# Seven products for eight: Strassen's method in the last block's up projection

## The chip, the cores and the metric

The kernel runs on one core of a Trainium2 chip. The metric is the device time of one execution in microseconds (us). TensorE (PE) multiplies, with weight loads (PEld) beside it; VectorE (DVE) and ScalarE (ACT) do elementwise work, GpSimd (POOL) some of it, and SyncE (SP) issues the DMAs between SBUF and DRAM. PE writes its results to PSUM, from where DVE and ACT take them.

## The reference

Three blocks run one after the other on a sequence of 1024 tokens of width 1024, all in float32. Two of their feed-forward parts are touched by the change. The first block's is a plain one; the third block's has a causal convolution of three taps between its two products and a gate:

```python
# first block
h2 = rms_norm(x, norm2_g[l])
up = jnp.square(jax.nn.relu(jnp.einsum('bsd,df->bsf', h2, w_up[l])))
x = x + jnp.einsum('bsf,fd->bsd', up, w_down[l])
...
# third block
def conv_ffn(h, w_up, conv_w, conv_b, w_down):
    u = h @ w_up
    C = u.shape[-1]
    u = lax.conv_general_dilated(
        u, conv_w.reshape(CONV_WIDTH_3, 1, C).astype(u.dtype), window_strides=(1,),
        padding=[(CONV_WIDTH_3 - 1, 0)], dimension_numbers=('NWC', 'WIO', 'NWC'),
        feature_group_count=C) + conv_b
    gate, val = jnp.split(u, 2, axis=-1)
    return (jax.nn.gelu(gate, approximate=True) * val) @ w_down
```

The rest (attention, retention, the mixed second block, the third block's attention and memory) is left as it was.

## The kernel before, in words

Activations lie as 8 tiles of 128 features, each over 1024 tokens, cut into two halves h of 512. A float32 product is made from three fp32r products: each operand is split into a high part (ACT rounds it: `whi`, `act`, `up`, `ws`) and a low part (the difference, on DVE or, with `pool_lo`, on POOL: `wlo` and the like), and `mm3` issues high x high, high x low and low x high. One dense unit (`dense`) is a 128-feature output chunk for one half: 8 x 3 = 24 matmuls of 128x512 into one PSUM bank. `chunk` loads a 512 KB weight chunk into `raw` and splits it into `whi` and `wlo`, two buffers of each; inside `third()` a third pair of `whi` and `wlo` is added in a pool of its own (`wx`).

The first FFN has 32 output chunks. Six are dense units, for h = 0 and then h = 1. The other 26 go in 13 Strassen units of two chunks: the two chunks are the rows of a 2 x 2 block matrix A, the two halves of the tokens the columns of B, and the inner dimension is cut in two. `right_forms` makes T1, T3 and T4 once, `left_forms` makes S1 to S4 of each unit (`sums`, split into `ws`), and `strassen` issues seven products of 4 x 3 = 12 matmuls, 84 a unit where dense units need 96. The four results are put together from PSUM by DVE additions (L820). `post` takes each: relu, square, and a write to DRAM (`upd`). The down product (`FfnDown`) reads `upd` back through two `nq` buffers, splits it, and runs over groups of 6, 6, 5, 5, 5, 5 chunks, each group adding its part to `acc`, which starts from x, loaded from `xd`.

The third FFN has 22 gate and 22 value chunks. `ffn` runs 6, 6, 5 and 5 pairs: for each half a gate unit, its convolution (ACT starts it with bias and the last tap, DVE adds two taps, and for h = 1 two small operations at the first columns with the `tail` of h = 0), gelu on ACT, a value unit, its convolution, the product on POOL, and the split into `up` in SBUF. The first group takes all of h = 0 first, since the norm of h = 1 (`join`, `norm_steps`) still runs beside it. Each group's down product follows it.

Nothing here writes the order of instructions by hand: a tile scheduler places each instruction on its engine's queue when the kernel is built, and slots, buffers and PSUM banks (six for products in a Strassen stage) decide what may start. Each engine then works through its queue in order.

## Time and profile before

| | |
|---|---|
| time, median of 3 runs | 3414.56 us (3406.56 to 3419.78) |
| profiled execution | 3415.66 us |
| its span, from the first to the last instruction | 3413.9 us |
| mean granted clock of TensorE | 0.975 |
| PE, PEld busy | 94%, 79% |
| DVE, ACT, POOL busy | 59%, 42%, 24% |
| first FFN (up and down) | about 580 to 1280 us of the span |
| third FFN (up and down) | about 2680 to 3390 us |

Matmuls are pipelined: one is shown about 0.39 us long, but the next starts earlier. The count of matmuls in a stretch, divided into its length, gives what one costs. A granted clock of 1.00 is TensorE's 2.4 GHz, 0.50 is 1.2 GHz.

### The profile page before, as it was taken

Reading aid. Unit: us, or ns where it says so; the run is one execution under the profiler, and the core shown is the slowest. Engines: PE = TensorE matmul, PEld = TensorE weight load, DVE = VectorE, ACT = ScalarE, POOL = GpSimd, SP = SyncE. Lnnn points to the kernel's source line nnn. Section 1 sums busy time; section 2 is a strip of 40 time slices with the busy share of each in tenths; the row PEclk is TensorE's granted clock in tenths of the full one; section 3 lists DMA queues with packets and bytes.
Section 4 is the critical chain, followed back from the end, with each engine's and each line's share of the span. In section 5 each row is a group of like instructions: output and inputs, shape, how many; then the busy total and the mean of one; then the engine's idle time right before and its main releaser. Section 6 shows DMA issues by size and latency. Waiting matters only on the chain.

```text
span 3413.9 us, 43231 instructions
## 1 busy us (share of the span) xinstructions
PE 3214.5 (94%) x16260; PEld 2679.9 (79%) x16260; DVE 2002.9 (59%) x3536; ACT 1427.8 (42%) x2512; POOL 822.2 (24%) x523
## 2 busy tenths in 40 slices
PE   7999999899999998789999899899999999999997
PEld 6789877788878887677667778778887888888886
DVE  8666566565443356975776566666636762434346
ACT  4454453454431124333644465655434542313132
POOL 3000024000000003521344444435333431201021
PEclk9999999999999999899999899999999999999999
DMA  4112134333352224345644122225322421111114
GB/s 129 46 52 63 51 112 160 121 121 114 127 183 81 78 70 154 99 123 179 203 162 135 59 63 67 82 86 177 131 68 99 154 85 58 45 50 46 51 43 149
DMA packets 144321, 348.18 MB, mean 102 GB/s; under 512 B 19441, under 2 KB 28017, under 8 KB 144113
## 3 DMA queue, kind: packets, MB, share of 16 engines
q1 hardware_dynamic: 144112, 345.42, 31.4%
q8 instruction: 128, 2.10, 0.3%
q14 instruction: 81, 0.66, 0.1%
HBM read 277.20 MB, written 61.34 MB: 99 GB/s over the span
## 4 chain that ended last, share of the span: by engine, by line
PE 40%; DVE 7%; issue 3%; ACT 3%; DMA 1%; POOL 1%; SPq 0%; DVEq 0%; POOLq 0%; ACTq 0%
PE ps_d L179 12%; PE ps_d L180 12%; PE ps_d L181 12%; ACT whi L143 1%; POOL wlo L145 1%; PE ps_s L1747 1%; PE ps_o L1330 1%; PE ps_t L1323 0%; DVE hE L1733 0%; DVE ssum L254 0%; DVE act L145 0%; DVE acc L1464 0%; DVE hSA L1748 0%; DVE wlo L145 0%; DVE acc L1465 0%
## 5 line engine op out<-in xcount | busy, mean ns | idle before, releaser
L179 PE MATMUL ps_d<-act,whi 128*128 128x512 f32 x1856 | 735.8, 397 | 22.7 <-ACT whi L143 10.2
L181 PE MATMUL ps_d<-act,wlo 128*128 128x512 f32 x1856 | 732.5, 395 | 17.4 <-DVE wlo L145 16.9
L180 PE MATMUL ps_d<-act,whi 128*128 128x512 f32 x1856 | 732.8, 395 | 0.1
L143 ACT ACTIVATE whi<-raw 128x1024 fp32r<-128x1024 f32 (+2 forms) x368 | 359.7, 978 | 779.9 <-PE ps_d L180 651.8
L145 POOL TENSOR_TENSOR wlo<-raw,whi 128x1024 fp32r<-128x1024 f32 (+1 forms) x162 | 391.1, 2418 | 747.2 <-ACT whi L143 712.9
L179 PEld LDWEIGHTS ps_d<-act,whi 128*128 128x128 f32 x1856 | 353.7, 191 | 100.7 <-ACT whi L143 17.2
L181 PEld LDWEIGHTS ps_d<-act,wlo 128*128 128x128 f32 x1856 | 353.2, 190 | 93.9 <-DVE wlo L145 20.9
L180 PEld LDWEIGHTS ps_d<-act,whi 128*128 128x128 f32 x1856 | 353.2, 190 | 72.7 <-issue 1.1
L179 PE MATMUL ps_d<-up,whi 128*128 128x512 f32 x864 | 337.2, 391 | 3.6 <-ACT whi L143 3.6
L181 PE MATMUL ps_d<-up,wlo 128*128 128x512 f32 x864 | 337.6, 391 | 1.7 <-DVE wlo L145 1.7
L180 PE MATMUL ps_d<-up,whi 128*128 128x512 f32 x864 | 337.0, 390 | 0.0
L145 DVE TENSOR_TENSOR wlo<-raw,whi 128x1024 fp32r<-128x1024 f32 (+2 forms) x206 | 230.2, 1117 | 168.1 <-ACT whi L143 164.7
L219 POOL TENSOR_TENSOR rr<-rv,mhalf 128x4 f32<-128x4 f32 (+1 forms) x43 | 46.4, 1080 | 716.4 <-DVE rv L209 530.2
L179 PE MATMUL ps_d<-mix,whi 128*128 128x512 f32 x512 | 200.1, 397 | 6.2 <-DVE acc L635 4.3
L181 PE MATMUL ps_d<-mix,wlo 128*128 128x512 f32 x512 | 200.8, 393 | 4.8 <-POOL wlo L145 4.8
L180 PE MATMUL ps_d<-mix,whi 128*128 128x512 f32 x512 | 202.3, 395 | 1.4 <-DVE mix L145 1.4
L179 PEld LDWEIGHTS ps_d<-up,whi 128*128 128x128 f32 x864 | 162.6, 188 | 38.5 <-ACT whi L143 4.9
L181 PEld LDWEIGHTS ps_d<-up,wlo 128*128 128x128 f32 x864 | 162.5, 188 | 36.9 <-DVE wlo L145 3.3
L180 PEld LDWEIGHTS ps_d<-up,whi 128*128 128x128 f32 x864 | 162.6, 188 | 33.9 <-DVE up L145 0.3
L179 PE MATMUL ps_d<-whi,act 128*128 128x256 f32 x512 | 151.4, 298 | 23.2 <-ACT act L379 16.0
L180 PE MATMUL ps_d<-wlo,act 128*128 128x256 f32 x512 | 150.2, 296 | 2.6 <-POOL wlo L145 1.6
L181 PE MATMUL ps_d<-whi,act 128*128 128x256 f32 x512 | 148.0, 292 | 0.1
(435 smaller groups left out, 6085.0 us busy)
## 6 DMA issues: line engine op xcount, KB each, us to landing
raw<-in_w_up SPq DMA_DIRECT2D x94, 512.0 KB, 3.4
raw<-in_w_fm SPq DMA_DIRECT2D x84, 512.0 KB, 3.4
raw<-in_w_out SPq DMA_DIRECT2D x42, 512.0 KB, 3.4
xd<-acc SPq DMA_DIRECT2D x80, 256.0 KB, 2.6
raw<-in_w_down SPq DMA_DIRECT2D x64, 320.0 KB, 3.0
nq<-upd SPq DMA_DIRECT2D x64, 256.0 KB, 3.0
acc<-xd SPq DMA_DIRECT2D x64, 256.0 KB, 5.7
raw<-in_w_down SPq DMA_DIRECT2D x32, 384.0 KB, 3.1
```

Of the source, the lines that this page charges most:

```text
L143: nc.scalar.activation(hi, src, AF.Copy)
L145: e.tensor_tensor(lo, src, hi.bitcast(F32), op=ALU.subtract)
L179: nc.tensor.matmul(out, lhsT=wh, rhs=xh, start=start, stop=False, skip_group_check=more)
L180: nc.tensor.matmul(out, lhsT=wh, rhs=xl, start=False, stop=False, skip_group_check=more)
L181: nc.tensor.matmul(out, lhsT=wl, rhs=xh, start=False, stop=stop, skip_group_check=more)
L219: self.nc.gpsimd.tensor_tensor(r, v, self.mhalf.broadcast_to([P, n]), op=ALU.pow)
L1330: nc.tensor.matmul(po[32 * hd : 32 * hd + 32, :P], lhsT=va[ct][:, band + kb, blk(hd, 32)], rhs=pts[hd][:, blk(kb)], start=kb == 0, stop=kb ...
L1747: nc.tensor.matmul(s[:, blk(j, 64)], lhsT=x[:, blk(j)], rhs=xv[:, nb * j : nb * j + nb, 1], start=True, stop=True)
```

## The change

First FFN. The next weight chunk is loaded before the current dense unit is issued. The left forms of the first Strassen unit are begun in the last two dense units of h = 1 (before: from the fourth on), in tiles c of the stage's pool. `strassen` issues the seven products in another order. The first, A11·B11, is copied by ACT from its bank into a second one, so that the next products add to it in PSUM; the next unit's A11·B11 is issued between S3·T3 and A22·T4. A unit has two DVE additions instead of five, and three ACT copies out of or within PSUM instead of one. The down product no longer starts from x: group 0 is copied, and x is loaded in 256 KB pieces and added at group 2.

Third FFN. Four pairs stay dense, h = 0 first, and 18 go through `strassen`, the gate chunk and the value chunk of a pair as the two rows. Convolution, gelu and the product (now on DVE) are in `post`; the result is written to DRAM (`upd3`) and read back by `FfnDown` with groups 6, 6, 5, 5. All `wlo` of this stage are made by DVE. The norm and the right forms work in place. `third()` is closed ahead of the stage and opened again for the down product alone.

```diff
         forms, left = iter(()), iter(())
-        for h in range(2):
-            if h == 1:
+        units = [(f, h) for h in range(2) for f in range(n0)]
+        wc = e.chunk(io["w1_up"][0])
+        for i, (f, h) in enumerate(units):
+            if i == n0:
                 for _ in steps:
                     pass
-                forms, left = right_forms(e, acc, hs, fm), left_forms(e, weight, 0, w)
-            for f in range(n0):
-                act(f, h, e.dense(e.chunk(io["w1_up"][f]), hs[h]), tmp.tile([P, HALF], F32, tag="c", name="c"))
-                next(steps, None)
-                next(forms, None)
-                if f >= 3:
-                    next(left, None)
-        hs = None
+                xs = [[a[:, j] for a in acc] for j in range(2)]
+                acc.clear()
+                forms, left = right_forms(e, xs, hs, fm), left_forms(e, weight, 0, w, tmp)
+            p = e.dense(wc, hs[h])
+            if i + 1 < len(units):
+                wc = e.chunk(io["w1_up"][units[i + 1][0]])
+            act(f, h, p, tmp.tile([P, HALF], F32, tag="c", name="c"))
+            next(steps, None)
+            next(forms, None)
+            if h and f >= n0 - 2:
+                next(left, None)
+        hs = p = None
...
-        def post(u, c):
-            for (i, h), t in c.items():
-                act(n0 + 2 * u + i, h, *t)
+        def post(u, i, h, p):
+            act(n0 + 2 * u + i, h, p, tmp.tile([P, HALF], F32, tag="c", name="c"))
...
-    def add(f, h, p, first):
+    def add(f, h, p, g):
         if len(acc) == f:
             acc.append(e.slot("acc"))
-            nc.sync.dma_start(acc[f], xd[f])
+        if g == 0:
+            nc.scalar.activation(acc[f][:, h], p, AF.Copy)
+            return
         nc.vector.tensor_tensor(acc[f][:, h], p, acc[f][:, h], op=ALU.add)
+        if g == 2:
+            t = e.tsq()
+            nc.sync.dma_start(t, xd[f, :, h])
+            nc.vector.tensor_tensor(acc[f][:, h], acc[f][:, h], t, op=ALU.add)
...
-    for i, tag in enumerate(("raw", "whi")):
+    for tag in ("raw", "raw") if tmp else ("raw", "whi"):
         a.append(e.wp.tile([P, NK, P], F32, tag=tag, name="raw"))
-        nc.sync.dma_start(a[i], weight(u, i))
+        nc.sync.dma_start(a[-1], weight(u, len(a) - 1))
     (a11, a12), (a21, a22) = ((t[:, :4], t[:, 4:]) for t in a)
-    s12, s34 = (e.wp.tile([P, 2, 4, P], F32, tag="wlo", name="sums") for _ in range(2))
+    def pair():
+        if tmp is None:
+            t = e.wp.tile([P, 2, 4, P], F32, tag="wlo", name="sums")
+            return t[:, 0], t[:, 1]
+        return [tmp.tile([P, HALF], F32, tag="c", name="c").rearrange("p (a b) -> p a b", a=4) for _ in range(2)]
     def put(name, t):
         y = e.slot("ws", (2, 4, P), F32R)
...
         w[name] = y
     put("A11", a11)
-    nc.vector.tensor_tensor(s12[:, 0], a21, a22, op=ALU.add)
-    nc.vector.tensor_tensor(s12[:, 1], s12[:, 0], a11, op=ALU.subtract)
-    put("S2", s12[:, 1])
+    s1, s2 = pair()
+    nc.vector.tensor_tensor(s1, a21, a22, op=ALU.add)
+    nc.vector.tensor_tensor(s2, s1, a11, op=ALU.subtract)
+    put("S1", s1)
     yield
+    put("S2", s2)
     put("A12", a12)
-    nc.vector.tensor_tensor(s34[:, 0], a11, a21, op=ALU.subtract)
-    put("S3", s34[:, 0])
     yield
-    put("S1", s12[:, 0])
+    s3, s4 = pair()
+    nc.vector.tensor_tensor(s3, a11, a21, op=ALU.subtract)
+    nc.vector.tensor_tensor(s4, a12, s2, op=ALU.subtract)
+    put("S3", s3)
+    yield
     put("A22", a22)
+    put("S4", s4)
     yield
-    nc.vector.tensor_tensor(s34[:, 1], a12, s12[:, 1], op=ALU.subtract)
-    put("S4", s34[:, 1])
-    yield
...
-    plan = (("A11", "B11", 0), ("S2", "T2", 1), ("A12", "B21", 0), ("S3", "T3", 1), ("S1", "T1", 2), ("A22", "T4", 1), ("S4", "B22", 2))
+    def product(p, w, a, b, start, last):
+        y, x = w.pop(a), fm.pop(b) if last else fm[b]
+        for k in range(4):
+            e.mm3(p, (y[:, 0, k], y[:, 1, k]), (x[k][:, 0], x[k][:, 1]), start and k == 0, k == 3, True)
+    def first(w, last):
+        ps = [e.pd() for _ in range(3)]
+        product(ps[0], w, "A11", "B11", True, last)
+        nc.scalar.activation(ps[1], ps[0], AF.Copy)
+        return ps
+    ps = first(w, n == 1)
     for u in range(n):
         last = u == n - 1
         nxt = {}
         pre = iter(()) if last else left_forms(e, weight, u + 1, nxt)
-        ps = [e.pd() for _ in range(3)]
...
-                p1 = e.tsq()
-                nc.scalar.activation(p1, ps[0], AF.Copy)
-                u2 = add(e.tnt(), ps[1], p1)
-                post(u, {(0, 0): (ps[0], new())})
-                u3 = add(new(), ps[1], p1)
-                u3 = add(u3, ps[2], u3)
-                post(u, {(1, 1): (u3, u3)})
-                p1 = add(p1, ps[1], p1)
-                post(u, {(1, 0): (p1, p1)})
-                u2 = add(u2, ps[2], u2)
-                post(u, {(0, 1): (u2, u2)})
...
+        def step():
+            next(pre, None)
...
+        product(ps[2], w, "S1", "T1", True, last)
+        c22 = e.tsq()
+        nc.scalar.activation(c22, ps[2], AF.Copy)
+        step()
+        product(ps[1], w, "S2", "T2", False, last)
+        c12 = e.tnt()
+        nc.scalar.activation(c12, ps[1], AF.Copy)
+        step()
+        product(ps[0], w, "A12", "B21", False, last)
+        post(u, 0, 0, ps[0])
+        step()
+        product(ps[1], w, "S3", "T3", False, last)
+        nc.vector.tensor_tensor(c22, ps[1], c22, op=ALU.add)
+        step()
+        follow = None if last else first(nxt, u + 2 == n)
+        product(ps[1], w, "A22", "T4", False, last)
+        post(u, 1, 0, ps[1])
+        post(u, 1, 1, c22)
+        step()
+        product(ps[2], w, "S4", "B22", False, last)
+        nc.vector.tensor_tensor(c12, ps[2], c12, op=ALU.add)
+        post(u, 0, 1, c12)
+        step()
+        w, ps = nxt, follow
     for _ in then:
         pass
-def ffn(e, groups, up_w, up, down_src, add, end, steps, per=1):
...
+    steps = join(1, ms, xs, g_cpost, g_fpre, xd3, hn[1], True)
+    third.close()
+    e.psum_split(d=6, s=0, o=0)
+    upd = e.dram.tile([22, P, 2, HALF], F32, name="upd3")
...
-    def up(f, h, ws):
-        cg = e.tsq()
-        conv(f, e.dense(ws[0], hs[h]), h, cg)
-        nc.scalar.activation(cg, cg, AF.Gelu_apprx_tanh)
-        cv = e.tnt()
-        conv(22 + f, e.dense(ws[1], hs[h]), h, cv)
-        nc.gpsimd.tensor_tensor(cv, cg, cv, op=ALU.mult)
-        y = e.slot("up", dt=F32R)
-        e.split(y[:, 0], y[:, 1], cv)
-        return y
-    def add(f, h, p, first):
+    def conv_rest(b, c):
+        c4 = lambda i: cw[:, 4 * b + i : 4 * b + i + 1]
+        t = tails.pop(b)
+        nc.vector.scalar_tensor_tensor(c[:, 0:1], t[:, 1:2], c4(1), c[:, 0:1], op0=ALU.mult, op1=ALU.add)
+        nc.vector.scalar_tensor_tensor(c[:, 0:2], t, c4(0), c[:, 0:2], op0=ALU.mult, op1=ALU.add)
+    def gelu(f, h, p, c):
+        conv(f, p, h, c)
+        if h:
+            conv_rest(f, c)
+        nc.scalar.activation(c, c, AF.Gelu_apprx_tanh)
+    def put_up(f, h, g, v):
+        nc.vector.tensor_tensor(v, g, v, op=ALU.mult)
+        nc.sync.dma_start(upd[f, :, h], v)
+    with ExitStack() as c2:
+        tmp = c2.enter_context(tc.tile_pool(name="str", bufs=8))
+        new = lambda: tmp.tile([P, HALF], F32, tag="c", name="c")
+        n0 = 4
+        fm, w = {}, {}
+        weight = lambda u, i: io["w3_up"][n0 + u + 22 * i]
+        forms, left = iter(()), iter(())
+        units = [(b, h) for h in range(2) for f in range(n0) for b in (f, 22 + f)]
+        wc = e.chunk(io["w3_up"][0])
+        for i, (b, h) in enumerate(units):
+            if i == 2 * n0:
+                for _ in steps:
+                    pass
+                forms, left = right_forms(e, xn, hs, fm), left_forms(e, weight, 0, w, tmp)
+            p = e.dense(wc, hs[h])
+            if i + 1 < len(units):
+                wc = e.chunk(io["w3_up"][units[i + 1][0]])
+            c = new()
+            if b < 22:
+                gelu(b, h, p, c)
+                cg = c
+            else:
+                conv(b, p, h, c)
+                if h:
+                    conv_rest(b, c)
+                put_up(b - 22, h, cg, c)
+            for _ in range(3):
+                next(steps, None)
+            next(forms, None)
+            if h and i >= len(units) - 2:
+                next(left, None)
+        hs = hn = p = c = cg = None
+        for _ in left:
+            next(forms, None)
+        for _ in forms:
+            pass
+        cs = {}
+        def post(u, i, h, p):
+            f = n0 + u
+            c = new()
+            if i == 0:
+                gelu(f, h, p, c)
+            else:
+                conv(22 + f, p, h, c)
+                if h:
+                    conv_rest(22 + f, c)
+            cs[i, h] = c
+            if i != h:
+                put_up(f, h, cs.pop((0, h)), cs.pop((1, h)))
+        down = FfnDown(e, (6, 6, 5, 5), upd, io["w3_down"])
+        strassen(e, tmp, fm, 22 - n0, weight, post, w, down.load(0))
+        fm.clear()
...
-    rest = ffn(e, (6, 6, 5, 5), lambda f: (e.chunk(io["w3_up"][f], pool_lo=True), e.chunk(io["w3_up"][22 + f])), up, io["w3_down"], add, end, steps_b, 4)
-    for _ in rest:
-        pass
-    third.close()
+    with e.third():
+        for _ in down.run(add, end):
+            pass
```

The scheduler sets the order anew, and three places of it are shown; the number behind a name is the buffer's. First, DVE in the first FFN, from the last `act` low parts (right forms, hs[1]) to the first left forms. Before:

```order
L145 TENSOR_TENSOR wlo_5878<-raw_5875,whi_5877 128x1024
L145 TENSOR_TENSOR wlo_5922<-raw_5919,whi_5921 128x1024
L145 TENSOR_TENSOR ws_6013<-raw_6007,ws_6013 128x512
L145 TENSOR_TENSOR wlo_5966<-raw_5963,whi_5965 128x1024
L787 TENSOR_TENSOR sums_6011<-raw_6009 128x512
L788 TENSOR_TENSOR sums_6011<-sums_6011,raw_6007 128x512
L145 TENSOR_TENSOR ws_6018<-sums_6011,ws_6018 128x512
L145 TENSOR_TENSOR act_6056<-acc_4750,act_6056 128x512
L145 TENSOR_TENSOR ws_6059<-raw_6007,ws_6059 128x512
L145 TENSOR_TENSOR wlo_6024<-raw_6021,whi_6023 128x1024
L792 TENSOR_TENSOR sums_6012<-raw_6007,raw_6009 128x512
L798 TENSOR_TENSOR sums_6012<-raw_6007,sums_6011 128x512
```

After:

```order
L145 TENSOR_TENSOR act_6048<-acc_4750,act_6048 128x512
L145 TENSOR_TENSOR wlo_5865<-raw_5862,whi_5864 128x1024
L145 TENSOR_TENSOR wlo_5909<-raw_5906,whi_5908 128x1024
L145 TENSOR_TENSOR wlo_5953<-raw_5950,whi_5952 128x1024
L145 TENSOR_TENSOR wlo_5997<-raw_5994,whi_5996 128x1024
L145 TENSOR_TENSOR wlo_6041<-raw_6038,whi_6040 128x1024
L145 TENSOR_TENSOR ws_6055<-raw_6051,ws_6055 128x512
L805 TENSOR_TENSOR c_6058<-raw_6053 128x512
L806 TENSOR_TENSOR c_6059<-c_6058,raw_6051 128x512
```

Five `wlo` of dense units now stand together ahead of the left forms (`ws`, and L805, which was L787).

Second, DVE in the third FFN, where h = 0 ends: `rv` and L263 are the norm of h = 1, L762 makes right forms, `act` is a split of hs[1], `wlo_22798` belongs to the second dense unit of h = 1. Before, from the first scaling of h = 1:

```order
L263 SCALAR_TENSOR_TENSOR nq_22605<-acc_21996,g_ffn_pre_norm_3_14910,ps_t_22600 128x512
L263 SCALAR_TENSOR_TENSOR nq_22610<-acc_21996,g_ffn_pre_norm_3_14910,ps_t_22600 128x512
L145 TENSOR_TENSOR act_22607<-nq_22605,act_22607 128x512
L145 TENSOR_TENSOR act_22612<-nq_22610,act_22612 128x512
L263 SCALAR_TENSOR_TENSOR nq_22694<-acc_21997,g_ffn_pre_norm_3_14910,ps_t_22600 128x512
L145 TENSOR_TENSOR up_22691<-nt_22659,up_22691 128x512
L263 SCALAR_TENSOR_TENSOR nq_22699<-acc_21997,g_ffn_pre_norm_3_14910,ps_t_22600 128x512
L1904 SCALAR_TENSOR_TENSOR nt_22758<-ps_d_22759,g_ffn_conv_3_14917,nt_22758 128x511
L145 TENSOR_TENSOR act_22696<-nq_22694,act_22696 128x512
```

After, from the norm's `rv` (L263 comes in four rows for eight operations):

```order
L207 TENSOR_REDUCE rv_22574<-ps_t_22569 128x4
L209 TENSOR_SCALAR rv_22574<-rv_22574 128x4
L263 SCALAR_TENSOR_TENSOR acc_22043<-acc_22043,g_ffn_pre_norm_3_14965,ps_t_22579 128x512 x2
L263 SCALAR_TENSOR_TENSOR acc_22044<-acc_22044,g_ffn_pre_norm_3_14965,ps_t_22579 128x512 x2
L263 SCALAR_TENSOR_TENSOR acc_22045<-acc_22045,g_ffn_pre_norm_3_14965,ps_t_22579 128x512 x2
L263 SCALAR_TENSOR_TENSOR acc_22046<-acc_22046,g_ffn_pre_norm_3_14965,ps_t_22579 128x512 x2
L145 TENSOR_TENSOR wlo_22798<-raw_22795,whi_22797 128x1024
L762 TENSOR_TENSOR acc_21191<-acc_22043,acc_21191 128x512
L1898 SCALAR_TENSOR_TENSOR c_22762<-ps_d_22731,g_ffn_conv_3_14972,c_22762 128x511
L762 TENSOR_TENSOR acc_21191<-acc_22043,acc_21191 128x512
L145 TENSOR_TENSOR act_22585<-acc_22043,act_22585 128x512
L762 TENSOR_TENSOR acc_21192<-acc_22044,acc_21192 128x512
```

The first `act` difference stood behind two scalings, and now stands behind eight, a `wlo`, sums of the right forms and a start of a convolution.

Third, ACT where the third FFN's down product begins. Before, the first `acc` copy of the first group and what is around it (`up` is the last split of the group):

```order
L143 ACTIVATE whi_23452<-raw_23450 128x768
L1903 ACTIVATE nt_23321<-ps_d_23322,g_ffn_conv_3_14917 128x512
L143 ACTIVATE up_23353<-nt_23321 128x512
L1929 ACTIVATE acc_23381<-ps_d_23362 128x512
L143 ACTIVATE whi_23499<-raw_23497 128x768
L1929 ACTIVATE acc_23381<-ps_d_23383 128x512
L1929 ACTIVATE acc_23428<-ps_d_23409 128x512
L143 ACTIVATE whi_23546<-raw_23544 128x768
```

After, from the last Strassen unit on (the tiles c_25932, c_25940 and c_25969 are its last results, `nq` the values read back, `whi_25994` the first weight in the reopened pool, whose space the tiles c had):

```order
L143 ACTIVATE up_25948<-nq_25946 128x512
L143 ACTIVATE up_25953<-nq_25951 128x512
L143 ACTIVATE up_25980<-nq_25978 128x512
L1897 ACTIVATE c_25932<-ps_d_25757,g_ffn_conv_3_14972 128x512
L1897 ACTIVATE c_25940<-sq_25832,g_ffn_conv_3_14972 128x512
L1897 ACTIVATE c_25969<-nt_25856,g_ffn_conv_3_14972 128x512
L143 ACTIVATE up_25985<-nq_25983 128x512
L1914 ACTIVATE c_25969<-c_25969 128x512
L143 ACTIVATE whi_25994<-raw_25992 128x768
L1981 ACTIVATE acc_26017<-ps_d_25998 128x512
L143 ACTIVATE up_26021<-nq_26019 128x512
L143 ACTIVATE up_26046<-nq_26044 128x512
```

Where weights were split ahead of the last results, the first weight's high part now stands behind the conv starts and the gelu of the last unit.

## Rows read from the trace of the kernel before

**Rows 1.** Page, part 1: engine busy us (share of the span) xinstructions.
```profile
PE 3214.5 (94%) x16260; PEld 2679.9 (79%) x16260; DVE 2002.9 (59%) x3536; ACT 1427.8 (42%) x2512; POOL 822.2 (24%) x523
```

**Rows 2.** Windows by stage: us, busy us (xinstructions) per engine, PEclk, DMA.
```profile
644.00:700.00 56.00, 50.64 (x207) 40.35 (x206) 28.07 (x42) 27.23 (x45) 0.00 (x0) 0.94 0.43 141
700.00:945.00 245.00, 245.00 (x1081) 202.65 (x1080) 131.74 (x200) 122.25 (x207) 0.11 (x1) 1.00 0.37 121
945.00:1000.00 55.00, 49.64 (x206) 38.97 (x205) 24.97 (x36) 14.53 (x22) 0.00 (x0) 0.97 0.55 181
...
2680.00:2780.00 100.00, 99.66 (x448) 82.02 (x447) 77.79 (x116) 49.16 (x69) 45.35 (x24) 1.00 0.34 115
...
3030.00:3390.00 360.00, 360.00 (x1594) 298.09 (x1592) 155.26 (x255) 101.16 (x138) 56.79 (x35) 1.00 0.21 66
```

**Rows 3.** PE waits, 560 to 1000: us in total, times, longest.
```profile
PE ps_d L179 <- ACT whi L143: 9.0, 7, 3.4
PE ps_d L181 <- DVE wlo L145: 5.4, 5, 3.2
```

**Rows 4.** PE waits, 2660 to 3394 (third FFN).
```profile
PE ps_t L228 <- POOL rr L219: 0.3, 1, 0.3
```

**Rows 5.** Windows behind two long PE waits; PEclk is the granted clock.
```profile
665.90:672.70 6.80, 6.28 (x15) 4.79 (x15) 0.61 (x1) 0.50 (x1) 0.00 (x0) 0.50 0.36 118
...
1290.50:1300.70 10.20, 4.83 (x12) 3.81 (x12) 9.80 (x14) 3.83 (x7) 3.18 (x3) 0.50 0.55 177
```

**Rows 6.** Lines by form, third FFN: busy us, mean ns of one, idle before.
```profile
L179 PE MATMUL ps_d<-act,whi 128*128 128x512 f32 x704 | 273.7, 389 | 0.0
...
L145 POOL TENSOR_TENSOR wlo<-raw,whi 128x1024 fp32r<-128x1024 f32 x29 | 69.9, 2410 | 304.2 <-ACT whi L143 304.2
...
L145 DVE TENSOR_TENSOR wlo<-raw,whi 128x1024 fp32r<-128x1024 f32 x28 | 34.4, 1229 | 41.2 <-ACT whi L143 38.2 <-PE ps_d L180 2.9
L1903 ACT ACTIVATE nt<-ps_d,g_ffn_conv 128x512 f32<-128x512 f32 x44 | 33.8, 768 | 31.0 <-PE ps_d L181 31.0
...
L1904 DVE SCALAR_TENSOR_TENSOR sq<-ps_d,g_ffn_conv,sq 128x511 f32<-128x511 f32 x44 | 32.8, 745 | 24.6 <-ACT sq L1903 24.6
...
L145 DVE TENSOR_TENSOR up<-nt,up 128x512 fp32r<-128x512 f32 x44 | 30.4, 691 | 77.0 <-ACT up L143 77.0
...
L143 ACT ACTIVATE up<-nt 128x512 fp32r<-128x512 f32 x44 | 27.8, 631 | 133.5 <-POOL nt L1920 133.5
...
L143 ACT ACTIVATE whi<-raw 128x768 fp32r<-128x768 f32 x16 | 13.5, 846 | 53.4 <-PE ps_d L180 53.4
...
L1912 DVE SCALAR_TENSOR_TENSOR nt<-tail,g_ffn_conv,nt 128x2 f32<-128x2 f32 x22 | 4.5, 206 | 0.0
```

**Rows 7.** DVE timeline in the opening of the third FFN: start us, length us.
```profile
2736.99 1.21 DVE L145 TENSOR_TENSOR wlo<-raw,whi 128x1024 fp32r<-128x1024 f32 x1
2738.13 0.74 DVE L1904 SCALAR_TENSOR_TENSOR sq<-ps_d,g_ffn_conv,sq 128x511 f32<-128x511 f32 x1
2738.79 1.28 DVE L145 TENSOR_TENSOR act<-nq,act 128x512 fp32r<-128x512 f32 x2
2739.99 0.68 DVE L145 TENSOR_TENSOR up<-nt,up 128x512 fp32r<-128x512 f32 x1
...
2743.53 1.30 DVE L145 TENSOR_TENSOR act<-nq,act 128x512 fp32r<-128x512 f32 x1 [0.16 <-ACT act L143]
```

**Rows 8.** POOL timeline, same stretch.
```profile
2741.87 2.41 POOL L145 TENSOR_TENSOR wlo<-raw,whi 128x1024 fp32r<-128x1024 f32 x1 [5.02 <-ACT whi L143]
```

**Rows 9.** Page, part 6: DMA issues, KB each, median us to landing.
```profile
xd<-acc SPq DMA_DIRECT2D x80, 256.0 KB, 2.6
...
nq<-upd SPq DMA_DIRECT2D x64, 256.0 KB, 3.0
acc<-xd SPq DMA_DIRECT2D x64, 256.0 KB, 5.7
```

More of the change, by code (lines that the diff above doesn't have):

```diff
@@ L675, in block1 @@
         save_x(f, 1)
-    steps = e.norm_steps([a[:, 1] for a in acc], g2, EPS, hs[1], inplace=True)
+    steps = e.norm_steps([a[:, 1] for a in acc], g2, EPS, hs[1], 2, inplace=True)
     e.psum_split(d=6, s=0, o=0)
@@ L850, in strassen @@
                     next(then, None)
-        for _ in pre:
-            pass
-        w = nxt
+        product(ps[2], w, "S1", "T1", True, last)
[22 more added lines that the diff above has]
+        w, ps = nxt, follow
     for _ in then:
         pass
-def ffn(e, groups, up_w, up, down_src, add, end, steps, per=1):
-    f0 = 0
-    for g, n in enumerate(groups):
-        us = [[], []]
-        fs = range(f0, f0 + n)
-        order = [(f, h) for h in range(2) for f in fs] if g == 0 else [(f, h) for f in fs for h in range(2)]
-        for f, h in order:
-            if g == 0 or h == 0:
-                w = up_w(f)
-            if h == 1:
-                for _ in steps:
-                    pass
-            us[h].append(up(f, h, w))
-            for _ in range(per):
-                next(steps, None)
-        last = g == len(groups) - 1
-        order = [(f, h) for h in range(2) for f in range(NK)] if last else [(f, h) for f in range(NK) for h in range(2)]
-        for f, h in order:
-            if last or h == 0:
-                w = e.chunk(down_src[f][:, f0 : f0 + n], (n, P))
-            add(f, h, e.dense(w, us[h]), g == 0)
-            for _ in range(per):
-                next(steps, None)
-            if last and f == NK - 1:
-                for _ in steps:
-                    pass
-                steps = end(h)
-        f0 += n
-    return steps
 class FfnDown:
@@ L1806, in join @@
         yield from add_x(e, ms, xs, g, r, [dst[k, :, h] for k in range(NK)], True)
-        yield from e.norm_steps(ms, g_next, EPS3, out, 1)
+        yield from e.norm_steps(ms, g_next, EPS3, out, 1, inplace)
     ms1 = tiles8(e)
@@ L1926, in add @@
+    def add(f, h, p, g):
         if acc[f] is None:
             acc[f] = e.slot("acc")
-        if first:
+        if g == 0:
             nc.scalar.activation(acc[f][:, h], p, AF.Copy)
```

45 lines of the change are left out of this document (11 added, 34 removed).

## The prediction

> **What bounds the kernel now.** I read the engine shares first [rows 1]: PE is busy 94% of the span, DVE 59% and ACT 42%, so PE's work and PE's waits make the time. Then the table by stage [rows 2]. Third FFN, from 3030 on: PE is busy all of 360 us at the full clock (2.4 GHz), and 360.00 / 1594 matmuls = 0.2258 us each. PE's waits in the whole stage sum to 0.3 us [rows 4]. So there time is the number of matmuls: that stage can gain only by fewer matmuls and lose only by new waits. First FFN: its Strassen units (700 to 945) have no gap, its two ends have. 207 matmuls x 0.2258 = 46.7 us stand in 56 us before them, 206 x 0.2258 = 46.5 in 55 us behind them: 9.3 and 8.5 us lost. The waits name ACT's whi and DVE's wlo, up to 3.4 and 3.2 us [rows 3]. An idle PE also lost clock: the grant was 0.50 (1.2 GHz) for 6.8 us after the longest of them, and for 10.2 us behind a wait in the second block [rows 5]. In 6.8 us it did 15 matmuls where 30 fit: 3.4 us.
>
> The sums stand against the profiled execution (3415.66 us, its span 3413.9 and 1.8 around it); the median is 1.1 lower.
>
> **Matmuls: -48.8 us.** Before, the third up product is 22 pairs x 2 rows x 2 halves x 24 = 2112 matmuls, three lines of 704 each (one of them in [rows 6]). After, 4 pairs stay dense (384) and 18 take seven products of 12 (18 x 84 = 1512): 216 fewer, x 0.2258 = 48.8 us.
>
> **Does DVE keep up in a Strassen unit? Taken: yes, 0 us.** PE needs 84 x 0.2258 = 19.0 us a unit. DVE gets 7 low parts and 4 sums of the weights, 2 PSUM additions and 2 products with gelu (15 of 128x512), 8 conv operations and 6 small ones (ends and tails). Back to back such operations start 0.60 us (128x512) and 0.66 us (conv) apart, though each is shown 0.68 and 0.74 long [rows 7]: 15 x 0.60 + 8 x 0.66 + 6 x 0.21 = 15.5 us, 82% of 19.0. With the mean lengths [rows 6] it is 15 x 0.69 + 8 x 0.745 + 6 x 0.21 = 17.6 us, 93%. Both fit. ACT gets 7 high parts, 3 PSUM copies, 4 conv starts and 2 gelus; at the longest of these lengths [rows 6], 16 x 0.77 = 12.3 us. POOL has nothing left in the stage, while before its work held DVE up: an act difference beside a POOL wlo took 1.30 us [rows 7, 8], where an up of the same size takes 0.69 on average [rows 6]. The Trainium skill ("SBUF — State Buffer", section "Who interferes with whom") has a reason: a DVE instruction with two SBUF inputs contends with a GpSimd one that reads SBUF. By that rule the lengths fall without POOL, and the trace's 1.30 beside 0.69 agrees.
>
> **The turn from h = 0 to h = 1: +20 us (bounds 4 and 28).** Before, 12 dense units (65 us) stood between the last cross-attention product and the first use of hs[1], and POOL made half of the wlo (29 beside DVE's 28 [rows 6]). Now there are 8 (8 x 24 x 0.2258 = 43.4 us), DVE makes every wlo (1.23 us [rows 6], 1.14 to the next start [rows 7]), and the right forms wait behind the same norm. As the order of DVE shows, behind the rv of the norm stand 8 scalings, a wlo, sums of the right forms and a conv start before the first act difference. I count from the first dense unit, with the spacings above: rv at 43.4; POOL's rr, its transposition and its spreading, an estimate of 3.0, to 46.4; 8 x 0.66 to 51.7; wlo to 52.8; four more to 55.4. PE has been done with h = 0 since about 45: about 10 us idle, then half clock. DVE then has ten operations to 61.4 (the other act parts, which units 9 and 10 take in turns), and 12 us of right forms, conv and products before the wlo of unit 11: 74.4. Without waits PE would have started that unit at 10 x 5.42 = 54.2. So 20 us are lost there; the half clock lies inside it, since DVE is late by itself. The lower bound is what remains if DVE's neighbours overlap better (a wait of 4 us); the upper adds 7 us for a second fall of the clock and the late wlo of unit 12.
>
> **The end of the Strassen units: +18 us (bounds 4 and 22).** down.run opens the third pair of weight buffers in the space that the tiles c had, and its first whi goes there. So that whi waits until the last products have been written to DRAM. The order of ACT shows it behind the three conv starts and the gelu of the last unit, and PE has nothing else to do. From the last Strassen matmul (0): two pairs of up values have yet to go through the two nq buffers in front of the conv starts on ACT, each turn 3.0 (transfer [rows 9]) + 0.63 + 0.69 = 4.3 us, of which half lies under PE's last 24 matmuls: 4.2. Three conv starts, six conv operations, two products and a low part follow on DVE to 11.9; the write of 256 KB, taken as 2.6 like xd<-acc [rows 9], to 14.5; whi 128x768 0.85 [rows 6] to 15.4. Then half clock for 6.8 us or more [rows 5]: +3. The lower bound is a write that lands early with nothing queued before it; the upper takes 10.2 us at half clock.
>
> **First FFN: -10 us (bounds 0 and -18).** At 644 to 700 the wlo of the last dense units stood between the left forms on DVE, and ACT's whi behind the ws of sums that waited for a weight. Now five wlo follow each other ahead of the left forms: I take 7 of 9.3 us. Behind the units, 8 loads acc<-xd (5.7 us each [rows 9]) leave SP's queue, but the two nq buffers still feed the up values one by one: 3 of 8.5 us. In the units DVE loses 3 of 5 additions and ACT gains 2 copies; PE has no gap there [rows 2], so 0. The stall at 621 to 627 hangs on norm and right forms, whose order stays: 0. The x values, added at group 2 by 16 loads and additions beside the down product: 0, for PE waits for nothing there; without that cover 16 x 0.69 = 11 us of DVE.
>
> **Sum:** -48.8 + 20 + 18 - 10 = -20.8: 3415.7 - 20.8 = 3394.9, and from the median 3393.8; I write 3394.
>
> **Rivals.** (A) Both new waits are small, since what DVE and SP have in front of them runs earlier than I count. For it: PE waits 0.3 us in the stage now, though DVE is busy 78 of 100 us at the same turn [rows 2, 4]. Against: the queues shown in the orders. 4 + 4 instead of 38: -48.8 + 8 - 12 = -53, 3362.
> (B) Not faster, no loss: the waits reach their upper bounds and the first FFN gives nothing: -48.8 + 28 + 22 = +1, 3415. For it: every row on the norm and nq chains has a wait behind it; against: three things must come together.
> (C) Slower: DVE becomes the bound inside the units. The place is the addition of S3·T3 (c22), which has to read its bank before A22·T4 may write there: if DVE is late, PE waits in every unit. 17.6 us by mean lengths leave 1.4 us for waits on ACT and PE at 16 handovers; 0.2 us each pass it. From 1.2 us of wait a unit (20.8 / 18) the gain is gone; at 2.5 it is 18 x 2.5 = 45: 3439. Against: DVE lengths overlap [rows 7]. The Trainium skill ("Perfetto Trace Analysis", "Identifying the Most-Contended Engine") takes the share of busy time as a fair measure of how near Vector is to its limit; by it 93% would leave almost nothing. Rows 7 disagree in size: starts are closer than lengths.
> (D) The change does not do what it says, the two halves' conv or the copies in PSUM undoing the saved products: 216 matmuls less are in the program, so only a wait could do it, and that is (C).
>
> **How the numbers follow.** Forecast 0.52, its own range 3378 to 3410; A 0.24; B 0.12; C 0.12. The measurement tells 0.5% (17 us) from no change, so faster means below 3397.5. Of the forecast some 0.30 lies below that and 0.22 above; A is all faster; B is the same, with 0.02 slower; C is 0.03 same and 0.09 slower. Faster 0.54, same 0.35, slower 0.11. The range leaves the lower part of A and most of C out: 3360 to 3420.
>
> **What would show it.** The matmul count of the third up product falls by 216 and its units hold 0.226 us a matmul: right on the first two steps; PE gaps at each addition of c22: C. Two gaps of about 10 us with the grant at 0.50 behind them, one 45 us after the stage's first matmul and one at the first down matmul, the second with PE waiting for ACT's whi and this for the write upd3<-c: right on the next two. Gaps under 3 us there would make the prediction wrong on the low side. In the first FFN the waits at 644 to 700 should be gone and those behind the units still be there.

## The result

The changed kernel takes 3396.8 us (median of 5 runs, 3391.8 to 3399.1) beside 3414.5: a ratio of 0.995 with the 95% interval 0.9936 to 0.9964, 12 to 22 us less. The forecast was 3394. The profiled execution took 3399.1 us with a span of 3397.3, against 3415.7 and 3413.9.

The profile after, engine shares first (as [rows 1]):

```profile
PE 3174.9 (93%) x16044; PEld 2645.4 (78%) x16044; DVE 2119.8 (62%) x3795; ACT 1504.1 (44%) x2710; POOL 698.0 (21%) x451
```

216 PE instructions are gone (16260 to 16044), DVE has 117 us more, POOL 124 less. The windows by stage, columns as in [rows 2]:

```profile
644.00:700.00 56.00, 54.92 (x241) 44.80 (x240) 30.69 (x46) 31.28 (x54) 0.00 (x0) 1.00 0.47 152
925.00:980.00 55.00, 55.00 (x245) 45.53 (x244) 14.16 (x19) 21.60 (x37) 0.11 (x1) 1.00 0.37 122
...
2714.00:2742.00 28.00, 15.21 (x57) 11.27 (x56) 27.11 (x44) 14.91 (x25) 0.12 (x1) 0.86 0.08 29
...
2780.00:3116.00 336.00, 334.71 (x1477) 276.83 (x1476) 272.08 (x512) 172.96 (x288) 0.00 (x0) 1.00 0.27 86
3116.00:3135.00 19.00, 6.02 (x17) 4.08 (x17) 11.77 (x23) 7.22 (x11) 0.00 (x0) 0.69 0.37 127
3134.48:3140.00 5.52, 5.52 (x13) 4.35 (x14) 0.94 (x1) 0.00 (x0) 0.00 (x0) 0.50 0.26 71
```

The first two are the ends of the first FFN's Strassen units: 241 matmuls in the 56 us that held 207, and behind the units 245 in 55 us, without a gap. The next three are the third FFN: at the turn of the halves 28 us hold 57 matmuls where 124 fit (28 / 0.2258), the Strassen units run at the full clock with DVE busy 272 of 336 us, and 19 us at their end hold 17 matmuls. The last is the half clock behind that. PE's waits in 560 to 1000 (us in total, times, longest; as [rows 3]) are left with the one at 622 that hangs on wlo, the two on acc at 580 and 599, which stood there before too, and small ones:

```profile
PE ps_d L181 <- DVE wlo L145: 3.2, 1, 3.2
PE ps_d L179 <- DVE acc L635: 3.0, 2, 2.2
PE ps_d L179 <- ACT whi L143: 0.9, 2, 0.5
```

In the third FFN, where PE waited 0.3 us in all [rows 4], these waits stand now (2655 to 3340):

```profile
PE ps_d L179 <- ACT whi L143: 12.8, 3, 11.0
PE ps_d L180 <- DVE act L145: 6.7, 1, 6.7
PE ps_d L181 <- DVE wlo L145: 3.9, 1, 3.9
PE ps_d L179 <- DVE sq L867: 1.9, 1, 1.9
PE ps_d L179 <- ACT act L143: 1.7, 1, 1.7
PE ps_d L179 <- ACT acc L1438: 1.5, 1, 1.5
PE ps_d L179 <- ACT ps_d L840: 1.3, 1, 1.3
```

**The turn.** DVE's timeline, start and length in us, at the 6.7 us wait on an act part and the 3.9 us one on a wlo:

```profile
2712.13 0.69 DVE L207 TENSOR_REDUCE rv<-ps_t 128x4 f32<-128x512 f32 x1
...
2714.89 5.36 DVE L263 SCALAR_TENSOR_TENSOR acc<-acc,g_ffn_pre_norm,ps_t 128x512 f32<-128x512 f32 x8 [1.87 <-PE ps_t L228]
...
2723.16 0.68 DVE L145 TENSOR_TENSOR act<-acc,act 128x512 fp32r<-128x512 f32 x1
...
2740.14 1.22 DVE L145 TENSOR_TENSOR wlo<-raw,whi 128x1024 fp32r<-128x1024 f32 x1
```

The rv comes 44.5 us after the first dense matmul (2667.68; forecast 43.4), the eight scalings begin 2.8 us later, the first act part follows at 2723.16, and unit 11's wlo at 2740.14, 17 us behind that, with DVE occupied nearly throughout. The dense units end at 2776.3: 108.6 us, of which 384 x 0.2258 = 86.7 are dense matmuls and 1.1 five early Strassen ones. The other 20.8 us are lost.

**The end.** ACT's timeline around the first down weight:

```profile
3122.73 0.63 ACT L143 ACTIVATE up<-nq 128x512 fp32r<-128x512 f32 x1 [0.91 <-DMA nq<-upd]
...
3130.13 0.63 ACT L1914 ACTIVATE c<-c 128x512 f32<-128x512 f32 x1 [3.95 <-DVE c L1908]
3133.59 0.84 ACT L143 ACTIVATE whi<-raw 128x768 fp32r<-128x768 f32 x1 [2.83 <-DMA upd<-c]
```

PE's timeline at the same place, its last Strassen matmul and its first down matmul:

```profile
3122.87 0.57 PE L181 MATMUL ps_d<-act,ws 128*128 128x512 f32 x1
3134.48 0.79 PE L179 MATMUL ps_d<-up,whi 128*128 128x512 f32 x1 [11.04 <-ACT whi L143]
```

The last up value ahead of the conv starts is split at 3122.73, these follow, then the gelu at 3130.13, and the whi waits 2.83 us for the write of c before it starts at 3133.59. PE stands from its last Strassen matmul (3122.87) to 3134.48 and then works at the half clock, 13 matmuls in 5.5 us. Before that it had waited 1.9 us for the addition of S3·T3 (L867, at 3118.09), which stood on DVE behind an up part that nq had delayed; first ACT's row, then DVE's:

```profile
3116.82 0.63 ACT L143 ACTIVATE up<-nq 128x512 fp32r<-128x512 f32 x1 [1.06 <-DMA nq<-upd]
...
3117.48 0.69 DVE L145 TENSOR_TENSOR up<-nq,up 128x512 fp32r<-128x512 f32 x1 [0.20 <-ACT up L143]
```

Together 1.9 + 1.6 (matmuls at half clock after it) + 11.2 (from one start to the next, less one matmul at that clock) + 2.6 (half clock behind it) = 17 us.

### The profile page after: what moved, and what is told of

Its sections match the earlier page's. It is cut to its first block, busy times and chain, and to the rows that moved or that the text cites. A ratio compares the mean times of both kernels' runs of the same rounds, so it can differ in the third digit from the quotient of the medians.

```text
span 3397.3 us, 43416 instructions
## 1 busy us (share of the span) xinstructions
PE 3174.9 (93%) x16044; PEld 2645.4 (78%) x16044; DVE 2119.8 (62%) x3795; ACT 1504.1 (44%) x2710; POOL 698.0 (21%) x451
## 4 chain that ended last, share of the span: by engine, by line
PE 35%; DVE 9%; ACT 3%; issue 2%; DMA 1%; POOL 1%; SPq 0%; DVEq 0%; ACTq 0%; POOLq 0%
PE ps_d L179 10%; PE ps_d L180 10%; PE ps_d L181 10%; ACT whi L143 1%; DVE act L145 1%; DVE acc L1454 1%; POOL wlo L145 1%; PE ps_s L1737 1%; DVE hE L1723 0%; DVE wlo L145 0%; DVE hSA L1738 0%; DVE acc L1455 0%; DVE pr L1650 0%; DVE ssum L254 0%; PE ps_o L1320 0%
## 5 line engine op out<-in xcount | busy, mean ns | idle before, releaser
L143 ACT ACTIVATE whi<-raw 128x1024 fp32r<-128x1024 f32 (+2 forms) x328 | 317.3, 968 | 711.6 <-PE ps_d L180 601.9
L179 PE MATMUL ps_d<-act,whi 128*128 128x512 f32 x1280 | 512.8, 401 | 24.5 <-DVE acc L316 8.1
L181 PE MATMUL ps_d<-act,wlo 128*128 128x512 f32 x1280 | 508.4, 398 | 20.4 <-DVE wlo L145 19.5
L180 PE MATMUL ps_d<-act,whi 128*128 128x512 f32 x1280 | 508.9, 398 | 6.8 <-DVE act L145 6.7
L145 POOL TENSOR_TENSOR wlo<-raw,whi 128x1024 fp32r<-128x1024 f32 (+1 forms) x134 | 326.0, 2436 | 446.4 <-ACT whi L143 427.9
L179 PE MATMUL ps_d<-act,ws 128*128 128x512 f32 x868 | 335.0, 390 | 3.8 <-DVE sq L867 1.9
L180 PE MATMUL ps_d<-act,ws 128*128 128x512 f32 x868 | 338.4, 390 | 0.0
L181 PE MATMUL ps_d<-act,ws 128*128 128x512 f32 x868 | 336.2, 390 | 0.0
L179 PEld LDWEIGHTS ps_d<-act,whi 128*128 128x128 f32 x1280 | 245.8, 192 | 80.8 <-ACT whi L143 14.6
L145 DVE TENSOR_TENSOR wlo<-raw,whi 128x1024 fp32r<-128x1024 f32 (+2 forms) x194 | 212.6, 1096 | 148.8 <-ACT whi L143 148.7
L181 PEld LDWEIGHTS ps_d<-act,wlo 128*128 128x128 f32 x1280 | 245.3, 192 | 73.9 <-DVE wlo L145 22.6
L180 PEld LDWEIGHTS ps_d<-act,whi 128*128 128x128 f32 x1280 | 245.7, 192 | 57.6 <-DVE act L145 7.5
L179 PEld LDWEIGHTS ps_d<-up,whi 128*128 128x128 f32 x864 | 163.0, 189 | 45.6 <-ACT whi L143 11.7
L179 PEld LDWEIGHTS ps_d<-act,ws 128*128 128x128 f32 x868 | 163.2, 188 | 38.7 <-ACT ps_d L840 2.7
L181 PEld LDWEIGHTS ps_d<-act,ws 128*128 128x128 f32 x868 | 163.3, 188 | 34.1
```

The lines of the kernel that those rows point to most:

```text
L143: nc.scalar.activation(hi, src, AF.Copy)
L145: e.tensor_tensor(lo, src, hi.bitcast(F32), op=ALU.subtract)
L179: nc.tensor.matmul(out, lhsT=wh, rhs=xh, start=start, stop=False, skip_group_check=more)
L180: nc.tensor.matmul(out, lhsT=wh, rhs=xl, start=False, stop=False, skip_group_check=more)
L181: nc.tensor.matmul(out, lhsT=wl, rhs=xh, start=False, stop=stop, skip_group_check=more)
```

## The experiments

Each was run beside the kernel before: the whole change in one series of measurements, the others in three more. The ratios and 95% intervals are those on record; the two medians of a row divide to within 0.0009 of them. The last two columns are lengths in us from one trace of each kernel: the first FFN from the wait at 622 to the one ahead of the second block, the third FFN from its first matmul to the end of the span. Where the code is the same they repeat well: the four kernels with the third FFN as in the whole change have 729.6 to 730.0.

| run | median us | before, same series | ratio | first FFN | third FFN |
|---|---|---|---|---|---|
| before | 3414.5 | | | 664.3 | 741.0 |
| whole change | 3396.8 | 3414.5 | 0.9950 [0.9936, 0.9964] | 647.7 | 729.6 |
| first_only | 3400.0 | 3410.9 | 0.9967 [0.9954, 0.9979] | 647.2 | 741.2 |
| third_only | 3406.1 | 3410.9 | 0.9983 [0.9973, 0.9992] | 661.3 | 729.6 |
| end_turn | 3383.7 | 3410.9 | 0.9921 [0.9908, 0.9933] | 647.6 | 719.5 |
| dense6 | 3397.8 | 3410.9 | 0.9959 [0.9945, 0.9972] | 647.8 | 730.0 |
| pool_lo | 3397.2 | 3412.1 | 0.9961 [0.9948, 0.9973] | 646.3 | 733.6 |
| no_sums | 3387.1 | 3412.1 | 0.9928 [0.9915, 0.9940] | 647.9 | 723.6 |
| end_lazy | 3376.6 | 3412.1 | 0.9896 [0.9881, 0.9911] | 647.4 | 712.3 |
| lazy_pool | 3382.4 | 3412.1 | 0.9913 [0.9900, 0.9927] | 647.2 | 715.9 |
| acc_load | 3398.2 | 3408.9 | 0.9962 [0.9945, 0.9978] | 649.7 | 730.0 |
| old_loop | 3398.5 | 3408.9 | 0.9961 [0.9946, 0.9975] | 653.6 | 729.8 |
| lazy5 | 3373.0 | 3408.9 | 0.9889 [0.9875, 0.9904] | 647.7 | 710.4 |

**The two parts apart.** first_only keeps the third block as before; third_only keeps block1 and its helpers.

> First FFN changed, third FFN as before. Theory (the first FFN's waits at both ends of its Strassen units go, 16 to 17 us in the traces, and the matmul count stays): 3414.5 - 17 = 3398 us, as fast as the whole change, with no PE gap over 1 us between 640 and 1260 us. Rival (part of these 17 us is the clock's luck in one execution, my forecast of -10 being right): 3405 us.

> Third FFN changed, first FFN as before. Theory (216 matmuls x 0.2258 = -49 us, then +21 at the turn of the halves and +18 at the first down matmul): 3414.5 - 10 = 3404 us, and the two PE gaps of about 7 and 11 us stand there again. Rival (the order in the untouched second and third block, which the scheduler laid anew, costs the 10 us that the whole change lost between the two FFNs): 3414 us, no gain at all.

first_only is 11 us faster (7 to 16), third_only 5 (3 to 9): together about the whole, 17. In time first_only lies nearer to its rival, and third_only between theory and rival. The traces side with the theory of first_only: the first FFN takes 647.2 us there, 647.7 in the whole change and 664.3 before. But third_only, whose first FFN has the instructions of before in the same order, took 661.3, so some 3 of these 17 us are chance of one execution. third_only shows the waits of 6.7 and 11.0 us again, and its third FFN is 11.4 us shorter than before, of which 5 are lost again just ahead of it ("Why the prediction was right"). Its rival does not hold: between the two FFNs its instructions come in the order of before, and this stretch, from the wait ahead of the second block to the last cross-attention, takes 1330.1 us there and 1334.1 before. So most of the 49 us that the third FFN saved in matmuls it gave back inside itself.

**The end.** end_turn moves the rotation of the weight buffers by one; end_lazy opens the pool after the third chunk.

```diff
 # end_turn
+    e.turn = 2
     with e.third():
         for _ in down.run(add, end):
 # end_lazy: c3 = ExitStack(), opened inside add
+        if (g, f, h) == (0, 2, 1):
+            c3.enter_context(e.third())
...
-    with e.third():
-        for _ in down.run(add, end):
-            pass
+    for _ in down.run(add, end):
+        pass
```

> The whole change, but the down product's first two weights go to the two old buffers and only the third to the reopened pool. Theory (PE's 11 us stand there because the first weight's buffer lies where the tiles c were, so its high part waits for their last write to DRAM): the gap at the first down matmul falls from 11.0 to 3 us or less, with less half clock behind it, 3397 - 12 = 3385 us. Rival (PE would then wait as long for the up values, which come one pair at a time through the two nq buffers): the gap stays over 8 us and the time at 3395 us.

> The whole change, the third pool opened only after the third chunk of the down product. Theory (any weight put into the space of the tiles c waits for their last write): neither the 11 us wait at the first down matmul nor the 3.8 us one that was left 8 us later when only the turn was moved: 16 us faster than the whole change, 3 to 4 faster than with the turn moved. Rival (with two buffers for the first weights each waits for PE to give one back): a wait of 2 us or more at the second to fourth weight, no faster than with the turn moved.

PE's waits in end_turn, 2655 to 3340:

```profile
PE ps_d L180 <- DVE act L145: 6.7, 1, 6.7
PE ps_d L179 <- ACT whi L143: 5.0, 2, 3.8
PE ps_d L181 <- DVE wlo L145: 3.6, 1, 3.6
```

The same view of end_lazy:

```profile
PE ps_d L180 <- DVE act L145: 6.7, 1, 6.7
PE ps_d L181 <- DVE wlo L145: 3.8, 1, 3.8
...
PE ps_d L179 <- ACT whi L143: 1.6, 2, 1.1
```

The 11 us are gone at once in end_turn, and a wait of 3.8 stands where the third weight, now the first in the pool, comes up (3131). In end_lazy this goes too. The 1.9 us on L867 are listed in neither: in both, 25 down matmuls now stand ahead of the last Strassen product and cover it. The gain of end_lazy over the whole change is 0.9896 against 0.9950, 18 us (11 to 25 by the two intervals) and 17.3 in the third FFN of the traces, where the sum had put +18 on this end. The rival, that the up values through nq hold PE, would have kept the wait: it went with the buffer's place alone.

**The turn.** no_sums leaves out the 16 subtractions of the third FFN's right forms; pool_lo gives every second wlo to POOL; dense6 has six dense pairs.

```diff
 # no_sums (in right_forms, third FFN alone; so too for b12, b22, b21)
-        nc.vector.tensor_tensor(b11, b12, b11, op=ALU.subtract)
+        sums and nc.vector.tensor_tensor(b11, b12, b11, op=ALU.subtract)
 # pool_lo
-                wc = e.chunk(io["w3_up"][units[i + 1][0]])
+                wc = e.chunk(io["w3_up"][units[i + 1][0]], pool_lo=i % 2 == 1)
 # dense6 (lazy5: 5, on end_lazy)
-        n0 = 4
+        n0 = 6
```

> The whole change without the 16 subtractions that make T1, T3 and T4 in the third FFN (this leaves out part of the computation: the products are made from unsummed tiles), so DVE has 16 x 0.60 = 9.6 us less to do at the turn. Theory (DVE's queue): three of them stand ahead of the first act parts, so the first wait falls from 6.7 to about 5 us, and the second, on unit 11's wlo, goes: the opening's 21 us fall to about 14. Rival (the chain of the norm itself, rv, rr, spreading and the scalings, sets the turn): both waits stay within 1 us of what they were.

PE's waits in no_sums, the row for the act part:

```profile
PE ps_d L180 <- DVE act L145: 5.4, 1, 5.4
```

The wait falls from 6.7 to 5.4 us, the one on unit 11's wlo is gone, and the dense units take 102.5 us (2664.1 to 2766.5) instead of 108.6: 6 of the 16 x 0.60 = 9.6 us taken off DVE come back. So DVE's queue is shown as the cause of 6 of the 20.8 us. What is left stands behind the norm and its eight scalings, which this run did not touch.

> The whole change with POOL making the wlo of every second dense unit of the third FFN. Theory (at the turn DVE's queue is the bound, and the second wait, 3.9 us on the wlo of unit 11, stands behind 17 us of right forms and act parts): that wlo leaves the queue, the second wait goes or shrinks to 2 us at unit 12, the first one (6.7 us on act) stays: the opening's 21 us fall to about 15, 6 us less than the whole change. Rival (POOL's reads hold DVE up as they did before, 1.30 instead of 0.69 us a difference, and a wlo takes 2.4 us there): no gain or 3 us slower.

It was the rival, and worse: PE now waits 5.1 us for a wlo of POOL, and the dense units take 113.3 us instead of 108.6. The medians don't tell pool_lo from the whole change, but its third FFN is 4.0 us longer. POOL's timeline, two wlo of one size:

```profile
2702.08 2.40 POOL L145 TENSOR_TENSOR wlo<-raw,whi 128x1024 fp32r<-128x1024 f32 x1 [7.11 <-ACT whi L143]
...
2731.93 5.75 POOL L145 TENSOR_TENSOR wlo<-raw,whi 128x1024 fp32r<-128x1024 f32 x1 [23.75 <-ACT whi L143]
```

DVE's timeline, the first row beside the first of them, the others beside the second:

```profile
2702.99 2.03 DVE L1917 TENSOR_TENSOR c<-c 128x512 f32<-128x512 f32 x1
...
2733.58 1.89 DVE L145 TENSOR_TENSOR act<-acc,act 128x512 fp32r<-128x512 f32 x3
...
2736.04 1.66 DVE L1907 SCALAR_TENSOR_TENSOR c<-tail,g_ffn_conv,c 128x1 f32<-128x1 f32 x1
```

The first wlo took 2.40 us, and DVE's product beside it 2.03 instead of 0.69. The second took 5.75 beside DVE's act parts, and a one-column conv tail of DVE, some 0.2 us elsewhere, took 1.66. The Trainium skill ("SBUF — State Buffer", "Who interferes with whom") calls the port pair of the two an exclusive lock; the trace agrees in that both lose. Beside the first wlo and beside DVE's act parts the one that started second lost. What the expectation had not weighed is that this can be the helper, and then it loses most: 3.35 us on one instruction.

> The whole change with six dense pairs instead of four, 16 Strassen units instead of 18. Theory (PE runs out of dense work of h = 0 before the norm of h = 1 and DVE's queue behind it are done; four more units of 5.4 us cover it): 24 more matmuls, +5 us, and the turn's 21 us fall to 5 or less: 3397 + 5 - 16 = 3386 us. Rival (DVE has more work in the opening than PE, each dense unit adding 1.1 of wlo and 1.4 of convolution to it, so the wait only moves): the turn still costs 15 us or more, 3397 us or above.

PE's waits for a wlo in dense6:

```profile
PE ps_d L181 <- DVE wlo L145: 6.2, 3, 5.4
```

The wait for an act part is gone, but 5.4 us on a wlo stand two units behind the start of h = 1, and the time is that of the whole change (0.9959 beside 0.9950, a third FFN of 730.0 beside 729.6 us). The dense units take 147.2 us, 16.0 more than their matmuls and the five early Strassen ones need. The theory had taken PE's cover for the remedy; the rival named what happened.

> Both together. Theory (two waits at two places, each with its own cause): the gains add, 16 + 6 = 22 us faster than the whole change. Rival (they overlap, since DVE is late throughout and the units only catch up): 16 us or less.

lazy_pool joins end_lazy and pool_lo. In their common series its median is 5.8 us above that of end_lazy, and its fastest run (3379.9) is slower than the slowest of end_lazy (3377.8); its third FFN is 3.6 us longer. So POOL costs time here as it did in pool_lo. Against the whole change lazy_pool is 13 us faster by the ratios, under the 16 of its rival, but not for the rival's reason: the 6 us that the theory took for pool_lo were not there. The 11 us at the end stay away and POOL's wlo holds PE for 5.1 us as in pool_lo: the two places are independent.

> The third pool opened late, as in end_lazy, with five dense pairs instead of four. Theory (the turn costs what DVE's queue is late, and each further pair of h = 0 gives PE 10.8 us to cover it while DVE needs about 8 for it): 12 more matmuls, +2.7 us, and 3 to 4 us less waiting at the turn: within 2 us of end_lazy. Rival (the norm's chain is the bound and 10.8 us of cover take most of the 20 us): 6 us or more faster than end_lazy.

lazy5 is end_lazy with five dense pairs. PE's waits, 2655 to 3340:

```profile
PE ps_d L181 <- DVE wlo L145: 5.2, 3, 4.2
PE ps_d L179 <- ACT whi L143: 2.0, 2, 1.2
PE ps_d L180 <- DVE act L145: 1.5, 2, 1.1
```

The waits at the turn sum to 5.2 + 1.5 = 6.7 us where end_lazy has 6.7 + 3.8 = 10.5. The ratio is 0.0007 (2 us) better, which two overlapping intervals can't confirm; in the traces the third FFN is 1.9 us shorter. Both are within the 2 us of the theory. It is the fastest of the runs, 0.9889 of the kernel before: 36 us less by the medians of its series, and 0.6% under the change as given.

**The first FFN.** old_loop takes the dense loop of before, with left_forms(e, weight, 0, w) in the weight buffers; acc_load starts acc from x.

```diff
 # old_loop
-            p = e.dense(wc, hs[h])
-            if i + 1 < len(units):
-                wc = e.chunk(io["w1_up"][units[i + 1][0]])
+                act(f, h, e.dense(e.chunk(io["w1_up"][f]), hs[h]), tmp.tile([P, HALF], F32, tag="c", name="c"))
...
+                if f >= 3:
+                    next(left, None)
 # acc_load
+            nc.sync.dma_start(acc[f], xd[f])
-        if g == 0:
-            nc.scalar.activation(acc[f][:, h], p, AF.Copy)
-            return
```

> The whole change, but the first FFN's dense units load each weight when its unit is issued, and the first left forms begin in the fourth of six units in the weight buffers, as before. Theory (left forms between the wlo on DVE, and ws ahead of whi on ACT, made the waits at 644 to 700): the 3.4 us wait on ACT's whi and the small ones around it come back with their half clock, 8 to 9 us, 3397 + 8 = 3405 us. Rival (the reordered units need their first operands later than before, so the same queue hurts less): 2 us or less.

> The whole change, but the first FFN's down product starts from x again, by eight 512 KB loads. Theory (these loads, in SP's queue between the reads of the up values, made the waits behind the first FFN's Strassen units): the waits of 1 to 2 us come back after the last unit, about 8 us lost there of the 8.5 that the change won, 3397 + 8 = 3405 us. Rival (the new order of the last unit's products and fewer DVE additions took them away): no wait over 1 us between 920 and 1000 us, 3397 us.

PE's waits in 560 to 1000, in old_loop:

```profile
PE ps_d L179 <- ACT whi L143: 4.9, 4, 3.0
PE ps_d L181 <- DVE wlo L145: 3.7, 2, 3.2
```

And in acc_load:

```profile
PE ps_d L181 <- DVE wlo L145: 3.9, 2, 3.2
...
PE ps_d L179 <- ACT whi L143: 2.0, 3, 1.1
```

In old_loop the waits of 3.0, 0.5 and 0.9 us at 661 to 675 are back, and the first FFN takes 653.6 us instead of 647.7: the loop's order and the place of the first left forms had made them, 6 us where the theory had 8 to 9 and the rival 2. In time old_loop has 0.9961 of the kernel before and the whole change 0.9950, 4 us, which their intervals tell neither from 6 nor from nothing. In acc_load waits of 1.1 and 0.7 us return at 960 and the first FFN takes 649.7 us: 2 of the 8.5 us that were lost there before. So the loads were a small part. The new order of the last unit's products, with fewer DVE additions, is left as the larger one; no run undid it alone, so this is argued, not shown.

## Why the prediction was right

- Matmuls, -48.8: this was right. 216 are gone, and the units ran at the full clock.
- DVE keeps up in a unit: this was right. DVE is busy 272 us in 336, 81%, where the spacing had given 82% and the mean lengths 93%, and PE works 334.7 of the 336. Rival C did not come. The rule on the share of busy time (the Trainium skill, "Perfetto Trace Analysis", "Identifying the Most-Contended Engine") held with the share of this stage's own rows; with lengths that overlap it would have warned for nothing.
- The turn, +20: it was 20.8. PE stood 6.7 + 1.7 us at the act parts where 10 were taken. The 3.0 us for POOL's rr, its transposition and its spreading were an estimate for which the prediction gives no row; 2.8 passed from the start of the rv to the first scaling. The terms for the wlo of unit 11, 61.4 + 12, add to 73.4 and not to 74.4; it was done 73.7 us after the first dense matmul (2740.14 + 1.22 - 2667.68). no_sums shows DVE's queue as the cause of 6 us; for the rest it is read from DVE's timeline and not tested. Longer cover alone moves the wait (dense6).
- The end, +18: it was 17 in the trace, 18 by end_lazy. One step was in the wrong place: the two nq turns (4.2 us) were put between the last Strassen matmul and the conv starts. They had passed by then and cost 1.9 us earlier, at L867, with 1.6 us at the half clock behind it. That 3.5 us stand there for 4.2 is luck, since the prediction has no wait at that place.
- The first FFN, -10: this term was mis-sized. It was -16.6 in the profiled executions, -13.7 against the first FFN of third_only, and -11 by first_only's median, whose interval (7 to 16) takes in 10 and 13.7 but not 16.6. At 644 to 700 7.7 of the 9.3 us came where 7 were taken; behind the units all 8.5 where 3 were. There I had held the nq reads for the cause that stays, and they were not.
- Not in the sum: 5.2 us just ahead of the third FFN. From the first matmul behind the cross-attention's last transposition to the first dense matmul there are 55.1 us, 49.9 before; the other kernels with the new third FFN have 54.8 to 55.1, first_only 49.9. Two wlo of POOL there take 7.41 us beside a run of seven act differences of DVE, where before, beside two of them, POOL's took 5.18 and DVE's two 4.36. So PE waits 2.6 us instead of 1.8, and 0.7 for a whi, and has the half clock behind it, which it had not before. And the first dense matmul, in PSUM banks that are now opened anew, waits 1.5 us for the copies of L1438, in the waits above. POOL's timeline there, then DVE's:

```profile
2633.34 7.41 POOL L145 TENSOR_TENSOR wlo<-raw,whi 128x1024 fp32r<-128x1024 f32 x2 [13.41 <-PE ps_d L181]
...
2631.48 4.29 DVE L145 TENSOR_TENSOR act<-acc,act 128x512 fp32r<-128x512 f32 x7
```

Before:

```profile
2643.37 5.18 POOL L145 TENSOR_TENSOR wlo<-raw,whi 128x1024 fp32r<-128x1024 f32 x2 [13.11 <-PE ps_d L181]
...
2644.73 4.36 DVE L145 TENSOR_TENSOR act<-nq,act 128x512 fp32r<-128x512 f32 x2 [0.46 <-ACT act L143]
```

In the profiled executions the third FFN from its first matmul to the end takes 11.4 us less (its terms, -48.8 + 20.8 + 17 + 1.3 for the wait at L840, give -9.7; 1.7 are not assigned). With -16.6 for the first FFN, +5.2, and +6.5 for code that neither kernel touches (below), and -0.3 ahead of all, that is -16.6, the difference of the spans. The forecast was -20.8: the first FFN gave 6.6 us more, and 11.7 us that were not in the sum took them back and 5 more. The matmuls and the two new waits came in the size that was forecast; their reasons are shown or open as said above. That the total came so near is in part luck: the 6.6 us too few in the first FFN and the 5.2 us that were left out nearly cancel, and the 6.5 us are chance of one execution.

## What to carry to other kernels

When work is taken from the bound engine, write out the helper engines' queues at the two seams of the new stage: at its start, where preparations bunch, and at its end, where the next stage's first operand may need a buffer that the last results still hold. Here 38 of 49 us went there. Before work is given to another helper to shorten a queue, look in the trace how long that helper takes beside the engine it is to relieve.
